# The norm and the transposes of the second block's first half of the tokens, with its first weights, between the steps of the last down product

## The chip, the cores and the metric

The kernel runs on one core of a Trainium2 chip. Its time is that of one execution on the device, in microseconds (us). Five engines work from queues of their own and wait for each other on semaphores: TensorE (PE, with its weight loads as PEld), VectorE (DVE), ScalarE (ACT), GpSimd (POOL) and SyncE (SP). DMA transfers are issued from the queues of SP, ACT and POOL.

## The reference

Two transformer blocks over 1024 tokens with 1024 channels, in float32. At the place of the change the first block ends and the second begins:

```python
def first_block(x, ...):
    ...
        u = rmsnorm(h, norm_mlp_g[l]) @ w_up[l]
        h = h + jnp.square(jax.nn.relu(u)) @ w_down[l]
    return rmsnorm(h, norm_final_g)

def second_block(x, ln1_g, w_in, b_in, ...):
        h = rms_norm(x, ln1_g[l])
        z = h @ w_in[l] + b_in[l]
        q, k, v, u, y_branch, g_att, g_rec = jnp.split(z, SPLITS, axis=-1)
        ...
        u = centred_depthwise_conv(u, conv_w[l], conv_b[l])
        ...
        y_rec = ((h_fwd + h_bwd) * jax.nn.gelu(y_branch)) @ w_rec_o[l]
        mixed = jax.nn.sigmoid(g_att) * y_att + jax.nn.sigmoid(g_rec) * y_rec
        x = x + mixed @ w_out[l]
        h2 = rms_norm(x, ln2_g[l])
        x = x + jnp.square(jax.nn.relu(h2 @ w_ff1[l])) @ w_ff2[l]
    return rms_norm(x, lnf_g)
```

So two norms meet: the first block's last one gives x1, the residual of the second block, and the second block's first one gives what is multiplied with w_in.

## The kernel before

A float32 product is made of three TensorE products: each operand is split into a high part, which ACT makes (`split`, L128, or L131 with a factor), and a low part, the rest, which DVE makes (L129, L132); the low part of some weights is made by POOL (`b.wlo`). High by high, high by low and low by high are added up in a PSUM bank.

The down product of the feed-forward (`ff_down`) is computed with 7 block products instead of 8 (in the manner of Strassen), each of 16 steps. A step multiplies a 128x512 left part with a 128x512 right part in four tiles q of 128 tokens: 12 matmuls. `divide(n)` splits the parts of a step, two steps ahead, into a ring of three buffers a side (tag `part`). The last three steps of the last product are done tile by tile, so that the tiles end one after the other; their parts have places of their own (`last_parts`). What a product gives is added to the eight token tiles `h` (128 tokens x 1024) by DVE between the steps of the next (L1066). The last product gives its four sums to the first half of the channels of tokens 4 to 7 only; these additions are kept in `b.late`, and `finish` calls them later. Tokens 0 to 3 are therefore complete some steps into the last product.

`block2` then makes the norms, four tokens at a time. Per token ACT squares and sums (L1350), DVE multiplies by norm_final_g (`gf`, L1335), ACT squares and sums again (L1353). Both root factors come from `rsqrt`, Newton steps on 128x4 tiles on DVE (L247 to L258). One factor (`rr`) scales h into `xn` (DVE, L1364), the other (`r1`) makes x1 in place (ACT, L1365), which goes to DRAM for later. `to_T` transposes `xn` on TensorE, two tokens at a time, by way of the banks `tp` and `sc`, and splits the transposed piece into `xT`, scaled by ln1_g. For tokens 4 to 7 this is put into the background list and drained between y and u of the first half.

The first projections are `y_chunk(0)` (the branch through GELU) and `u_chunk(0)` (which goes to the recurrence), each once for tokens 0 to 3 (js = 0) and once for 4 to 7 (js = 1); each makes two outputs of 24 matmuls. Later comes a list of other chunks, the attention, the recurrence, the merge of both branches, and a second feed-forward with the same `ff_down`.

The scheduler orders instructions by priority as they are written; `high_priority(offset)` lets some come earlier, `issue_after` holds some behind a given instruction.

## Time and profile before

| what | value |
|---|---|
| three runs | 3052.94, 3053.9, 3058.38 us |
| median | 3053.9 us |
| profiled execution | 3052.53 us, span 3050.8 us |
| TensorE busy | 2900.2 us, 95% of the span |
| DVE busy | 2162.9 us, 71% |
| ACT busy | 1231.9 us, 40% |
| mean granted TensorE clock | 0.977 of full speed |

The span goes from the first to the last instruction of the profiled execution. A busy TensorE is not TensorE at its peak, since its clock changes: 1.0 is 2.4 GHz, 0.5 is 1.2 GHz. In the span the last down product of the first block runs from about 1451.3 to 1494.9 us, and the first chunk of projections of the second block ends at about 1584 us.

### The profile page before, as it was taken

What the parts mean: (1) busy time and instruction counts of PE and PEld (TensorE: products, weight loads), DVE (VectorE), ACT (ScalarE), POOL (GpSimd) and SP (SyncE); (2) the same over time, 40 slices, a digit from 0 to 9 for tenths busy, and PEclk for the clock granted to TensorE, in tenths of its full rate; (3) what the DMA queues carried; (4) which work ended last, traced back from release to release, by engine and by line L of the source; (5) the groups of instructions that cost most, each with busy time, mean ns of one, the idle gap of its engine ahead of it and who ended that gap; (6) DMA issues with size and microseconds to landing.
All of it is one profiled execution on the core that took longest, in us unless ns stands there. A gap on an engine that the chain in (4) does not pass through costs nothing.

```text
span 3050.8 us, 40049 instructions
## 1 busy us (share of the span) xinstructions
PE 2900.2 (95%) x14596; PEld 2440.8 (80%) x14596; DVE 2162.9 (71%) x3903; ACT 1231.9 (40%) x2272; POOL 369.5 (12%) x402
## 2 busy tenths in 40 slices
PE   7898899999999999999699999999999999999997
PEld 5798788788877788888577789888788878888886
DVE  6997777565587776996558787643445777669976
ACT  4122566242253223444556664543311432224444
POOL 2240110000012431000111222200000011100000
PEclk9999899999999999999899999999999999999999
DMA  3225564211124768642211323477843233366522
GB/s 127 61 79 161 176 193 123 97 42 55 44 103 158 231 205 319 224 156 78 96 68 49 125 89 111 154 201 225 283 150 97 97 105 111 112 234 246 186 90 83
DMA packets 252501, 422.86 MB, mean 139 GB/s; under 512 B 27893, under 2 KB 130832, under 8 KB 252304
## 3 DMA queue, kind: packets, MB, share of 16 engines
q1 hardware_dynamic: 214240, 305.86, 31.2%
q0 software_dynamic: 28832, 95.57, 9.1%
q10 hardware_dynamic: 9232, 18.88, 1.6%
q8 instruction: 115, 1.88, 0.3%
q14 instruction: 82, 0.67, 0.1%
HBM read 310.75 MB, written 111.69 MB: 138 GB/s over the span
## 4 chain that ended last, share of the span: by engine, by line
PE 79%; DVE 10%; DMA 4%; ACT 3%; issue 2%; POOL 1%; SPq 0%; DVEq 0%; ACTq 0%; POOLq 0%
PE fd L1179 20%; PE mm L206 18%; PE ff L1007 15%; PE mm L177 5%; PE mm L179 5%; PE mm L178 5%; DVE acc L421 2%; PE ff L990 2%; PE pv L667 2%; PE tp L733 2%; PE pv L1641 1%; PE tp L240 1%; POOL w L129 1%; DMA bt<-rpb_d 1%; ACT w L128 1%
## 5 line engine op out<-in xcount | busy, mean ns | idle before, releaser
L1179 PE MATMUL fd<-part,part 128*128 128x512 f32 x2688 | 613.2, 390 | 1.0 <-DVE part L129 1.0
L1179 PEld LDWEIGHTS fd<-part,part 128*128 128x128 f32 x2688 | 503.5, 188 | 110.3 <-DVE part L129 5.9
L1007 PE MATMUL ff<-x,w 128*128 128x512 f32 x2352 | 541.6, 392 | 13.0 <-ACT w L128 7.3
L206 PE MATMUL mm<-xh,w 128*128 128x512 f32 x1792 | 532.2, 394 | 1.5 <-ACT lruC L1513 1.3
L1007 PEld LDWEIGHTS ff<-x,w 128*128 128x128 f32 x2352 | 443.7, 189 | 110.6 <-ACT w L128 9.0
L206 PEld LDWEIGHTS mm<-xh,w 128*128 128x128 f32 x1792 | 336.7, 189 | 70.1 <-ACT lruC L1513 2.4
L128 ACT ACTIVATE part<-keep 128x512 fp32r<-128x512 f32 x384 | 223.8, 623 | 252.0 <-PE fd L1179 247.4
L206 PE MATMUL mm<-xl,w 128*128 128x512 f32 x896 | 316.5, 393 | 0.0
L129 DVE TENSOR_TENSOR part<-keep,part 128x512 fp32r<-128x512 f32 x384 | 249.2, 683 | 47.2 <-ACT part L128 47.0
L128 ACT ACTIVATE w<-raw 128x1024 fp32r<-128x1024 f32 (+1 forms) x132 | 134.9, 1033 | 282.6 <-PE mm L178 111.5
L129 POOL TENSOR_TENSOR w<-raw,w 128x1024 fp32r<-128x1024 f32 x56 | 170.9, 3056 | 493.7 <-ACT w L128 491.2
L206 PEld LDWEIGHTS mm<-xl,w 128*128 128x128 f32 x896 | 168.9, 189 | 33.6
L232 DVE TENSOR_TENSOR h<-h,mm 128x512 f32<-128x512 f32 x176 | 119.7, 685 | 78.7 <-PE mm L179 77.9
L421 DVE SCALAR_TENSOR_TENSOR acc<-u,conv_wh,acc 128x1023 f32<-128x1023 f32 (+14 forms) x120 | 172.6, 1477 | 3.1 <-ACT acc L416 1.3
L177 PE MATMUL mm<-w,xh 128*128 128x256 f32 x512 | 147.9, 289 | 14.9 <-DVE u L447 11.5
L850 DVE TENSOR_TENSOR t2k<-ff,t2k 128x512 f32<-128x512 f32 x140 | 96.3, 688 | 82.1 <-PE ff L1007 80.8
L178 PE MATMUL mm<-w,xh 128*128 128x256 f32 x512 | 147.0, 287 | 0.0
L179 PE MATMUL mm<-w,xl 128*128 128x256 f32 x512 | 146.8, 287 | 0.0
L128 ACT ACTIVATE w<-wr 128x512 fp32r<-128x512 f32 x156 | 94.3, 630 | 119.6 <-PE ff L1007 55.8
L972 POOL DMA_DIRECT2D hid_d<-t2k x128 | 69.8, 545 | 488.9 <-DVE t2k L850 256.0
L129 DVE TENSOR_TENSOR w<-raw,w 128x1024 fp32r<-128x1024 f32 (+1 forms) x76 | 89.2, 1179 | 47.1 <-ACT w L128 47.0
L129 DVE TENSOR_TENSOR w<-wr,w 128x512 fp32r<-128x512 f32 x156 | 104.4, 686 | 15.8 <-ACT w L128 14.0
(355 smaller groups left out, 5167.5 us busy)
## 6 DMA issues: line engine op xcount, KB each, us to landing
hid_d<-t2k POOLq DMA_DIRECT2D x128, 256.0 KB, 3.0
x<-hid_d SPq DMA_DIRECT2D x128, 256.0 KB, 4.4
keep<-hid_d SPq DMA_DIRECT2D x96, 256.0 KB, 6.0
raw<-in_w_in_dram SPq DMA_DIRECT2D x40, 512.0 KB, 3.7
qk_d<-t2k SPq DMA_DIRECT2D x64, 256.0 KB, 2.6
wr<-in_w_up_dram SPq DMA_DIRECT2D x32, 512.0 KB, 3.8
keep<-in_w_down_dram SPq DMA_DIRECT2D x64, 256.0 KB, 5.2
wr<-in_w_ff_dram SPq DMA_DIRECT2D x32, 512.0 KB, 3.6
```

The costliest lines, as they stand in the source:

```text
L128: nc.scalar.activation(hi, src, AF.Copy)
L129: (eng or nc.vector).tensor_tensor(out=lo, in0=src, in1=fp(hi), op=ALU.subtract)
L177: nc.tensor.matmul(ps, sh, mh, start=(i == 0), stop=False)
L178: nc.tensor.matmul(ps, sh, ml, start=False, stop=False)
L179: self.last = nc.tensor.matmul(ps, sl, mh, start=False, stop=(i == n - 1))
L206: self.last = nc.tensor.matmul(pj[j], a, b, start=(k == 0 and q == 0), stop=(k == nk - 1 and q == 2))
L232: self.added[t] = self.nc.vector.tensor_tensor(out=hs, in0=hs, in1=ps, op=ALU.add)
L421: nc.vector.scalar_tensor_tensor(out=acc[m][:, lo:hi], in0=u[m][:, lo + d : hi + d], scalar=w(k), in1=acc[m][:, lo:hi], op0=ALU.mult, op1= ...
L850: tt = lambda o, x, y, op: nc.vector.tensor_tensor(out=o, in0=x, in1=y, op=op)
L972: stored.append(nc.gpsimd.dma_start(out=hid[2 * c + f, :, j * 512 : (j + 1) * 512], in_=o))
L1007: b.last = nc.tensor.matmul(ps, l[:, k, :], r, start=(opens and k == 0 and q == 0), stop=(k == 3 and q == 2), skip_group_check=True)
L1179: last = nc.tensor.matmul(ps[q], l[:, sl], r, start=(c == 0 and x == 0), stop=(c == C - 1 and x == 2))
```

## The change

The norm of `block2` becomes a class, `Front`, whose parts are called at given steps of the last product, by a table `work` that `ff_down` takes: the load of gf and of the first weights four steps ahead of the product; the squares of token q at step q + 1; the roots at step 5; the scaling of token q at step q + 6; the transposes of channel block k, two blocks a step at steps 10 to 12, and blocks 6 and 7 behind tiles 0 and 1 of the last three steps; the splits of the first weights of y at steps 11 and 12. A transposed piece now holds four tokens (128x512 instead of 128x256), so there are 8 rounds per half instead of 16. The scaling works in place on h; x1 goes into slots of its own and is stored from the GpSimd queue instead of ACT's. gf and the first weights are loaded from the GpSimd queue instead of SP's. The parts of the last three steps lie in `k2` to `k7`. For tokens 4 to 7, `rest` makes the norm behind the product, and the transposes (`turns`) are written behind y and u of js = 0, where before they stood between y and u.

```diff
@@ -237,7 +237,8 @@
     def transposes(self, dst, srcs):
         for i, s in enumerate(srcs):
-            self.nc.tensor.transpose(dst[:, i * P : (i + 1) * P], s, self.ident)
+            last = self.nc.tensor.transpose(dst[:, i * P : (i + 1) * P], s, self.ident)
+        return last
     def rsqrt(self, v, n=1):
...
@@ -1159,13 +1161,14 @@
             divide(n + PART)
         if len(steps) - LAST <= n + LAST < len(steps):
             if not last_parts:
-                last_parts += [b.slot(q, (P, 2, 512), F32R, "part") for q in (24, 25, 30)]
                 last_parts += [
-                    b.kpool.tile([P, 2, 512], F32R, tag=f"k{q}", name=b.nm("part")) for q in (0, 1, 8)
+                    b.kpool.tile([P, 2, 512], F32R, tag=f"k{q}", name=b.nm("part")) for q in range(2, 8)
                 ]
             divide(n + LAST)
         if n < 0:
             continue
+        for fn in work.get(n - len(steps) + C, ()):
+            fn(h)
         p, c = steps[n]
         if c == 0:
             ps = [
@@ -1191,6 +1194,8 @@
                     for m in range(n, len(steps)):
                         last = products(m, q, steps[m][1])
                 b.last = last
+                for fn in work.get(("tile", q), ()):
+                    fn(h)
         if c == C - 1:
             def evac(q, i, j, ps=ps):
...
-def block2(b, h):
-    nc, i = b.nc, b.i
-    tt = lambda o, a, q, op: nc.vector.tensor_tensor(out=o, in0=a, in1=q, op=op)
-    stt = lambda o, a, s, q, p0, p1: nc.vector.scalar_tensor_tensor(out=o, in0=a, scalar=s, in1=q, op0=p0, op1=p1)
-    b.x1_d = b.dram.tile([S, D], F32, name="x1_d")
-    gf = b.slot(11, name="gf")
-    nc.sync.dma_start(out=gf, in_=i["norm_final_g"].partition_broadcast(P))
-    xT = b.halves(range(0, 8))
-    last = None
-    for g0 in range(0, NT, 4):
-        ys = []
-        v, rr = (b.small(8, n) for n in ("bv", "br"))
-        for q in range(4):
-            t = g0 + q
-
-            finish(b, t, last)
-            junk = b.t2k((P, 1024), BF16)
-            nc.scalar.activation(junk, h[t], AF.Square, accum_out=v[:, q : q + 1])
-            last = tt(h[t], h[t], gf, ALU.mult)
-            junk = b.t2k((P, 1024), BF16)
-            nc.scalar.activation(junk, h[t], AF.Square, accum_out=v[:, 4 + q : 5 + q])
-        v0, v1, rr = v[:, 0:4], v[:, 4:8], rr[:, 0:4]
+class Front:
+    def __init__(self, b):
+        self.b, self.nc = b, b.nc
+        self.last = None
+        self.work = {}
+        for c, fn in (
+            [(-4, self.load)]
+            + [(q + 1, lambda h, q=q: self.squares(h, q)) for q in range(4)]
+            + [(5, lambda h: self.roots())]
+            + [(q + 6, lambda h, q=q: self.scaled(h, q, (25, 28, 29, 30)[q])) for q in range(4)]
+            + [(10 + k // 2, lambda h, k=k: self.turn(h, 0, k, (b.sc, b.pv))) for k in range(6)]
+            + [(11 + q, lambda h, q=q: self.weight(q)) for q in range(2)]
+            + [(("tile", k - 6), lambda h, k=k: self.turn(h, 0, k, (b.sc, b.pv))) for k in (6, 7)]
+        ):
+            self.work.setdefault(c, []).append(fn)
+    def load(self, h):
+        b, nc = self.b, self.nc
+        b.x1_d = b.dram.tile([S, D], F32, name="x1_d")
+        self.gf = b.slot(24, name="gf")
+        nc.gpsimd.dma_start(out=self.gf, in_=b.i["norm_final_g"].partition_broadcast(P))
+        self.xT = b.halves(range(8, 16))
+        self.w, self.raw = [], []
+        for q in range(2):
+            self.raw.append(b.kpool.tile([P, 4, 256], F32, tag=f"k{q}", name=b.nm("raw")))
+            nc.gpsimd.dma_start(
+                out=self.raw[q],
+                in_=b.i["w_in_2"][0, q * 512 : (q + 1) * 512, 2560:2816].rearrange("(k p) n -> p k n", p=P),
+            )
+    def weight(self, q):
+        b = self.b
+        hi, lo = (b.slot(26 + 2 * q + s, (P, 4, 256), F32R, "w") for s in range(2))
+        b.split(hi, lo, self.raw[q])
+        self.w.append((hi, lo))
+    def weights(self, k, c0, c1):
+        hi, lo = self.w[k // 4]
+        return hi[:, k % 4, c0:c1], lo[:, k % 4, c0:c1]
+    def squares(self, h, t):
+        b, nc, q = self.b, self.nc, t % 4
+        if q == 0:
+            self.v, self.rr = (b.small(8, n) for n in ("bv", "br"))
+        junk = lambda: b.slot(25 if t < 4 else 4 + q, (P, 1024), BF16, "junk")
+        nc.scalar.activation(junk(), h[t], AF.Square, accum_out=self.v[:, q : q + 1])
+        self.last = nc.vector.tensor_tensor(out=h[t], in0=h[t], in1=self.gf, op=ALU.mult)
+        nc.scalar.activation(junk(), h[t], AF.Square, accum_out=self.v[:, 4 + q : 5 + q])
+    def roots(self):
+        b, nc = self.b, self.nc
+        tt = lambda o, a, q, op: nc.vector.tensor_tensor(out=o, in0=a, in1=q, op=op)
+        v0, v1, rr = self.v[:, 0:4], self.v[:, 4:8], self.rr[:, 0:4]
         nc.vector.tensor_scalar(out=v0, in0=v0, scalar1=1.0 / D, scalar2=EPS, op0=ALU.mult, op1=ALU.add)
-        r1 = b.rsqrt(v0, 4)
+        r1 = self.r1 = b.rsqrt(v0, 4)
         tt(rr, r1, r1, ALU.mult)
         tt(rr, rr, v1, ALU.mult)
         nc.vector.tensor_scalar(out=v1, in0=rr, scalar1=1.0 / D, scalar2=EPS, op0=ALU.mult, op1=ALU.add)
         tt(rr, b.rsqrt(v1, 4), r1, ALU.mult)
-        for q in range(4):
-            t = g0 + q
-            y = b.slot(12 + t if t < 4 else 22 + t, name="xn")
-            last = nc.vector.tensor_scalar(out=y, in0=h[t], scalar1=rr[:, q : q + 1], scalar2=None, op0=ALU.mult)
-            nc.scalar.activation(h[t], h[t], AF.Copy, scale=r1[:, q : q + 1])
-            nc.scalar.dma_start(out=b.x1_d[t * P : (t + 1) * P, :], in_=h[t])
-            ys.append(y)
-        for g in (g0, g0 + 2):
-            if g < 4:
-                with b.tc.issue_after(b.last.ins):
-                    b.to_T(ys[g : g + 2], g, b.g_ln1, xT)
-            else:
-                b.bg.append((0, lambda ys=ys[g - 4 : g - 2], g=g: b.to_T(ys, g, b.g_ln1, xT, 100)))
-    xT += b.halves(range(8, 16))
+    def scaled(self, h, t, at):
+        b, nc, q = self.b, self.nc, t % 4
+        x1 = b.slot(at, name="x1")
+        nc.scalar.activation(x1, h[t], AF.Copy, scale=self.r1[:, q : q + 1])
+        nc.gpsimd.dma_start(out=b.x1_d[t * P : (t + 1) * P, :], in_=x1)
+        nc.vector.tensor_scalar(out=h[t], in0=h[t], scalar1=self.rr[:, q : q + 1], scalar2=None, op0=ALU.mult)
+    def turn(self, h, j, k, banks):
+        b = self.b
+        ps = banks[k % 2]()
+        with b.tc.issue_after(b.last.ins):
+            b.last = b.transposes(ps, [y[:, k * P : (k + 1) * P] for y in h[4 * j : 4 * j + 4]])
+        b.split(*self.xT[j][k], ps, scale=b.g_ln1[:, k : k + 1])
+    def rest(self, h):
+        b = self.b
+        for t in range(4, NT):
+            finish(b, t, self.last)
+            self.squares(h, t)
+        self.roots()
+        for t in range(4, NT):
+            self.scaled(h, t, t)
+        def turns():
+            self.xT += b.halves(range(0, 8))
+            with b.tc.high_priority(offset=100):
+                for k in range(KT):
+                    self.turn(h, 1, k, (b.sc, b.tp))
+        return turns
+def block2(b, h, front):
+    nc, i = b.nc, b.i
+    tt = lambda o, a, q, op: nc.vector.tensor_tensor(out=o, in0=a, in1=q, op=op)
+    stt = lambda o, a, s, q, p0, p1: nc.vector.scalar_tensor_tensor(out=o, in0=a, scalar=s, in1=q, op0=p0, op1=p1)
+    turns = front.rest(h)
+    xT = front.xT
     b.wlo = nc.gpsimd
     w_in = i["w_in_2"][0]
...
@@ -1432,10 +1499,10 @@
         while step not in done:
             b.bg.popleft()[1]()
-    ws = {}
+    ws = {("y", 0): front.weights}
     def y_chunk(q, js=(0, 1)):
-        if js[0] == 0:
+        if js[0] == 0 and q:
             ws["y", q] = b.w_s(w_in[:, 2560 + q * 256 : 2560 + q * 256 + 256])
         for mm in range(2):
             m = 2 * q + mm
@@ -1559,9 +1626,9 @@
     b.banks = 3
     for js in ((0,), (1,)):
         y_chunk(0, js)
+        u_chunk(0, js)
         if js == (0,):
-            b.drain()
-        u_chunk(0, js)
+            turns()
     seq = [0, y_chunk, u_chunk, 0, y_chunk, 0, u_chunk, 0, y_chunk, 0, u_chunk] + [0] * (1 + 4)
     others = [(qk_chunk, p) for p in range(4)] + [(v_chunk, n) for n in range(2)] + [(gate_chunk, q) for q in range(4)]
     nth = {y_chunk: 1, u_chunk: 1}
@@ -1756,10 +1823,11 @@
         if stop not in ("mix",):
             cross_part(b, h)
         if stop not in ("mix", "cross"):
-            h = ff_part(b, h, b.g_mlp, ins["w_up"][0], ins["w_down"][0], bias_tables(b))
+            front = Front(b)
+            h = ff_part(b, h, b.g_mlp, ins["w_up"][0], ins["w_down"][0], bias_tables(b), front.work)
             b.layout(None)
         if stop not in ("mix", "cross", "ff"):
-            block2(b, h)
+            block2(b, h, front)
             h = merge_part(b)
         if stop is None:
             h = ff_part(b, h, b.g_ln2, ins["w_ff1_2"][0], ins["w_ff2_2"][0])
```

The first place is the end of DVE's work for the last product (`part` are its splits, `h_11250` to `h_11253` tokens 0 to 3, `sm` the root factors). Before, with all splits of the product already ahead of these rows:

```order
L1335 TENSOR_TENSOR sm_13787<-sm_13827,sm_13809 128x4
L1364 TENSOR_SCALAR xn_13843<-h_11250,sm_13787 128x1024
L1364 TENSOR_SCALAR xn_13847<-h_11251,sm_13787 128x1024
L1364 TENSOR_SCALAR xn_13851<-h_11252,sm_13787 128x1024
L1364 TENSOR_SCALAR xn_13855<-h_11253,sm_13787 128x1024
L1066 TENSOR_TENSOR h_11254<-h_11254,fd_13458 128x512
L132 SCALAR_TENSOR_TENSOR xl_13782<-sc_13864,cols_412,xh_13778 128x256
```

After:

```order
L1393 TENSOR_TENSOR sm_13500<-sm_13626,sm_13608 128x4
L1408 TENSOR_SCALAR h_11250<-h_11250,sm_13500 128x1024
L1408 TENSOR_SCALAR h_11251<-h_11251,sm_13500 128x1024
L129 TENSOR_TENSOR part_13706<-x_13598,part_13706 128x512
L129 TENSOR_TENSOR part_13709<-keep_11232,part_13709 128x512
L1408 TENSOR_SCALAR h_11252<-h_11252,sm_13500 128x1024
L129 TENSOR_TENSOR part_13730<-x_13654,part_13730 128x512
L129 TENSOR_TENSOR part_13733<-keep_11232,part_13733 128x512
L1408 TENSOR_SCALAR h_11253<-h_11253,sm_13500 128x1024
L129 TENSOR_TENSOR part_13754<-x_13679,part_13754 128x512
L129 TENSOR_TENSOR part_13757<-keep_11233,part_13757 128x512
L129 TENSOR_TENSOR w_13849<-raw_13386,w_13848 128x1024
```

The four scalings now stand among the splits of steps 10 (`part_13706`, `part_13709`), 11 and 12, in front of the part of a weight split that DVE makes; the additions of tokens 4 to 7 have moved behind.

The second place is TensorE between the product and the transposes (`fd` are the product's four banks, `ident` marks a transpose). Before, the end of the product's last tile:

```order
L1179 MATMUL fd_13461<-part_13677,part_13676 128x512 x3
L1179 MATMUL fd_13461<-part_13675,part_13674 128x512 x3
L1179 MATMUL fd_13461<-part_13673,part_13672 128x512 x3
L240 MATMUL sc_13864<-ident,xn_13843 128x128
L240 MATMUL sc_13874<-ident,xn_13843 128x128
L240 MATMUL sc_13864<-ident,xn_13847 128x128
L240 MATMUL sc_13874<-ident,xn_13847 128x128
L240 MATMUL sc_13884<-ident,xn_13843 128x128
```

After, the end of step 9 and the start of step 10 of the same product:

```order
L1182 MATMUL fd_13475<-part_13685,part_13682 128x512 x3
L1182 MATMUL fd_13476<-part_13685,part_13682 128x512 x3
L240 MATMUL sc_13770<-ident,h_11250 128x128
L240 MATMUL sc_13770<-ident,h_11251 128x128
L240 MATMUL sc_13770<-ident,h_11252 128x128
L240 MATMUL sc_13770<-ident,h_11253 128x128
L240 MATMUL pv_13777<-ident,h_11250 128x128
L240 MATMUL pv_13777<-ident,h_11251 128x128
L240 MATMUL pv_13777<-ident,h_11252 128x128
L240 MATMUL pv_13777<-ident,h_11253 128x128
L1182 MATMUL fd_13473<-part_13709,part_13706 128x512 x3
L1182 MATMUL fd_13474<-part_13709,part_13706 128x512 x3
```

Blocks 0 and 1 of all four tokens stand between two steps; blocks 2 and 3, and 4 and 5, do the same a step later each.

The third place is ACT in the norm of tokens 4 to 7 (`sm` here are the sums of squares; `w_` with `raw_` is the high part of a weight). Before:

```order
L1353 ACTIVATE t2k_13945,sm_13939<-h_11254 128x1024
L1350 ACTIVATE t2k_13948,sm_13939<-h_11255 128x1024
L131 ACTIVATE xh_13778<-tp_13859,cols_412 128x256
L128 ACTIVATE w_14377<-raw_14374 128x1024
L1353 ACTIVATE t2k_13951,sm_13939<-h_11255 128x1024
L131 ACTIVATE xh_13779<-tp_13869,cols_412 128x256
L1350 ACTIVATE t2k_13954,sm_13939<-h_11256 128x1024
L131 ACTIVATE xh_13780<-tp_13879,cols_412 128x256
L128 ACTIVATE w_14384<-raw_14381 128x1024
L1353 ACTIVATE t2k_13957,sm_13939<-h_11256 128x1024
```

After:

```order
L1389 ACTIVATE junk_13939,sm_13928<-h_11255 128x1024
L1387 ACTIVATE junk_13942,sm_13928<-h_11256 128x1024
L128 ACTIVATE w_14080<-raw_14078 128x1024
L128 ACTIVATE w_14086<-raw_14084 128x1024
L1389 ACTIVATE junk_13945,sm_13928<-h_11256 128x1024
L1387 ACTIVATE junk_13948,sm_13928<-h_11257 128x1024
L1518 ACTIVATE t2k_14036<-mm_14011,cols_412 128x512
L1519 ACTIVATE t2k_14037<-mm_14011,cols_412 128x512
L128 ACTIVATE w_14329<-raw_14326 128x1024
L1389 ACTIVATE junk_13951,sm_13928<-h_11257 128x1024
L1522 ACTIVATE t2k_14037<-t2k_14037 128x512
L128 ACTIVATE w_14336<-raw_14333 128x1024
```

The splits of transposed pieces (L131) have left this stretch. The two passes over the first output of y (L1518, L1519) and a weight split (`w_14329`) stand now in front of the second square of the last token (`junk_13951`).

## Rows read from the trace of the kernel before

**Rows 1.** page part 1: engine, busy us (share of the span), instructions

```profile
PE 2900.2 (95%) x14596; PEld 2440.8 (80%) x14596; DVE 2162.9 (71%) x3903; ACT 1231.9 (40%) x2272; POOL 369.5 (12%) x402
```

**Rows 2.** windows: us, busy per engine (instructions), PEclk, DMA share, GB/s

```profile
1451.30:1494.90 43.60, 43.58 (x193) 35.75 (x191) 21.53 (x31) 20.56 (x36) 0.54 (x1) 1.00 0.22 70
1494.87:1533.81 38.94, 8.57 (x29) 4.11 (x28) 25.91 (x54) 25.73 (x44) 14.59 (x7) 0.56 0.33 111
1584.00:1960.00 376.00, 367.15 (x1777) 308.41 (x1776) 278.99 (x264) 226.59 (x279) 90.92 (x41) 0.99 0.31 99
```

**Rows 3.** windows of five us: same columns

```profile
1495.00:1500.00 5.00, 0.00 (x0) 0.00 (x0) 1.64 (x1) 3.33 (x6) 4.62 (x2) 0.96 0.23 57
1535.00:1540.00 5.00, 5.00 (x21) 4.11 (x20) 4.07 (x23) 1.78 (x4) 0.00 (x0) 0.79 0.26 90
```

**Rows 4.** chain that ended last, 1480 to 1565: start, us, what

```profile
1479.92 14.29 PE fd L1179 x63
...
1494.24 2.00 ACT w L128 x2
...
1498.36 2.76 DVE h L1335
...
1502.43 2.35 DVE sm L248
...
1510.78 2.74 DVE xn L1364 x4
```

**Rows 5.** timeline of ACT, 1472 to 1495: start, us, what [idle before]

```profile
1475.88 0.63 ACT L128 ACTIVATE part<-x 128x512 fp32r<-128x512 f32 x1 [1.57 <-PE fd L1179]
1476.42 0.62 ACT L128 ACTIVATE part<-keep 128x512 fp32r<-128x512 f32 x1
...
1479.66 1.04 ACT L1350 ACTIVATE t2k<-h 128x1024 bf16<-128x1024 f32 x1
1480.61 0.19 ACT L1350 ACTIVATION_READ_ACCUMULATOR t2k<-h 128x1 f32 x1
```

**Rows 6.** timeline of DVE, 1472 to 1528

```profile
1476.55 0.69 DVE L129 TENSOR_TENSOR part<-x,part 128x512 fp32r<-128x512 f32 x1 [1.43 <-ACT part L128]
1477.16 0.69 DVE L129 TENSOR_TENSOR part<-keep,part 128x512 fp32r<-128x512 f32 x1
...
1480.83 1.23 DVE L1335 TENSOR_TENSOR h<-h,gf 128x1024 f32<-128x1024 f32 x1 [0.27 <-ACT t2k L1350]
...
1510.58 0.16 DVE L1335 TENSOR_TENSOR sm<-sm,sm 128x4 f32<-128x4 f32 x1
...
1526.87 0.68 DVE L1066 TENSOR_TENSOR h<-h,fd 128x512 f32<-128x512 f32 x1
```

**Rows 7.** timeline of POOL, 1494 to 1540

```profile
1495.38 4.65 POOL L129 TENSOR_TENSOR w<-raw,w 128x1024 fp32r<-128x1024 f32 x2 [7.82 <-ACT w L128]
1502.39 4.70 POOL L129 TENSOR_TENSOR w<-raw,w 128x1024 fp32r<-128x1024 f32 x2 [2.36 <-ACT w L128]
1526.69 2.36 POOL L129 TENSOR_TENSOR w<-raw,w 128x1024 fp32r<-128x1024 f32 x1 [19.60 <-ACT w L128]
```

**Rows 8.** timeline of ACT, 1494 to 1592

```profile
1511.56 1.15 ACT L1365 ACTIVATE h<-h,sm 128x1024 f32<-128x1024 f32 x1 [6.89 <-DVE xn L1364]
...
1583.95 0.69 ACT L1471 ACTIVATE u<-mm,cols 128x512 f32<-128x512 f32 x1 [3.47 <-PE mm L206]
```

**Rows 9.** chain, 1541 to 1556: a transpose pair at full clock

```profile
1546.45 0.22 PE tp L240 x2
```

**Rows 10.** DMA view: issues, KB each, median us to landing

```profile
h_d<-h POOLq DMA_DIRECT2D x16, 512.0 KB, 3.0
...
x_d<-h ACTq DMA_DIRECT2D x8, 512.0 KB, 2.6
...
raw<-in_w_in_dram POOLq DMA_DIRECT2D x8, 512.0 KB, 4.2
```

**Rows 11.** PE's waits, 1960 to 2240: us, times, longest

```profile
PE mm L206 <- DVE ev L1699: 4.9, 1, 4.9
```

6 lines of the change are left out of this document (3 added, 3 removed).

## The prediction

> **What bounds the kernel now.** I read the page's first part first: TensorE is busy 95% of the span [rows 1], so the kernel is a queue of matmuls and only places where TensorE stands still, or runs slowly, can give much. The windows show where. In the last down product TensorE is busy 43.58 of 43.60 us at full clock [rows 2]: 16 steps of 2.725 us, 192 matmuls of 0.227 us. Then comes the hole: from 1494.87 to 1533.81 it is busy 8.57 of 38.94 us at a mean clock of 0.56 [rows 2]. Behind it the projections of the second block run dense, 367 of 376 us [rows 2].
>
> The chain of waits says what fills the hole [rows 4]. The last product ends; a weight split that has waited for it holds ACT for 2.0 us; the rest of the norm of tokens 0 to 3 follows (the gain product, the roots, four scalings of 0.69 us); then transposes and splits take turns, then all that again for tokens 4 to 7. The first chunk's four outputs per half (y 0, y 1, u 0, u 1) are done when ACT takes the last of them at 1583.95 [rows 8]. So from the end of the product to there it is 1583.95 - 1494.87 = 89.1 us. The work in it that only TensorE can do is 192 matmuls x 0.227 = 43.6 us and 64 transposes x 0.11 [rows 9] = 7.0 us. What is left, 38.5 us, is the most that this place can return.
>
> **The change, part by part.** *First half of the norm.* ACT and DVE are busy 20.6 and 21.5 of the last product's 43.6 us [rows 2], so there is room. ACT gets 8 square passes of 1.14 [rows 5] and 4 copies of 1.15 [rows 8], 13.7 us; DVE gets 4 gain products of 1.23, 29 small operations that start 0.20 apart, and 4 scalings of 0.69 [rows 4, 6], 13.5 us; the first weights add two splits (ACT 1.0 each [rows 4], DVE about 1.2). That fits in sum, but the order of the rows decides. A step's split can start when the step three before it has ended (three buffers), and costs a pair on ACT of 1.16 and on DVE of 1.30 [rows 5, 6], together 2.0 us; it is needed 5.45 us after its start is allowed. Laying out the new rows of both engines with these durations, the splits of steps 2 to 9 are ready 0.7 to 1.9 us before TensorE wants them. So I charge nothing there; the cover is thin, and each us by which ACT runs later beyond it is a us of TensorE.
>
> *The first stall.* Eight transposes now stand between step 9 and step 10, and they need all four scaled tokens. Step 9 ends at 1451.3 + 10 x 2.725 = 1478.55. In my layout DVE has done step 9's split at 1475.2; then come 19 small operations x 0.20 = 3.8, two scalings 1.4, the split pair of step 10, 1.3, a scaling 0.7, the pair of step 11, 1.3, a scaling 0.7: 1484.4. The stall is then 5.8 us. If DVE were not behind at step 9 (ready 2.0 us after its buffers come free at 1470.4), all of it would be 2.8 us earlier: 3.0 us. I take 5.0, nearer the late end, since the order puts squares and three early splits of the last steps ahead of step 9's. Step 10's split is done before that, so it adds nothing.
>
> *The clock.* The mean granted clock was 0.96 in 1495 to 1500, with TensorE idle from 1494.87: at half speed for 0.4 us of the five, so it fell some 4.7 us after the last matmul. In 1535 to 1540 it was 0.79, so it was back after 2.1 us there, 3.3 us after dense work began at 1533.81 [rows 3]. A fall thus costs 3.3 / 2 = 1.7 us. A stall of 5.0 is on the edge; I charge 1.0, with 0 and 1.7 as bounds.
>
> *Transposes in the product.* 32 x 0.11 = 3.5 us, wholly added to the product, since TensorE was full there. Their splits (ACT and DVE 0.7 each) have one step or one tile of cover; k 4 waits for a bank that k 0's split frees, which waits on ACT for a weight split, and this for stores of the x1 copies into whose slots it writes. Stores take 3.0 us from the GpSimd queue where the ACT queue takes 2.6 [rows 10]. They go out by 1480 and land by 1483, and k 4 is due at about 1491: covered.
>
> *First chunk, first half.* 96 matmuls x 0.227 = 21.8 us can follow the product at once, since weights and transposed tokens are there.
>
> *The second stall.* Tokens 4 to 7 get their last addition only when the product's tiles end, and their norm must fit into these 21.8 us. Count from the product's end. ACT reaches the first square of token 7 at about 5.2 (two weight splits stand before it), then the two passes over the first output, which TensorE has ready at 5.4, then a split of u's zero-padded weights whose load can only start when POOL has finished another weight (5.5) and takes 3 to 4 us: so token 7's second square ends at 11.4. Of the 29 small operations 15 to all wait for it, 3.0 to 5.8 us; I take 4.2. But POOL now runs its two subtractions of 2.36 us beside them. Before, a gain product that started during POOL's pair took 2.76 instead of 1.23 us, and a pair of tiny operations 2.35 [rows 4, 6, 7]; an addition that reads the product's bank kept its 0.68 us while POOL worked [rows 6, 7]. So operations on SBUF alone wait for POOL's end, up to 5 us in all, and 4.5 with the part that lies before 11.4; three GELU operations (2 us) and four scalings (2.8) end at 24.9. The stall is 24.9 - 21.8 = 3.1 us. Without the meeting with POOL it is 0; with later loads, up to 8 and a fall of the clock. I take 3.0.
>
> *The rest.* 32 transposes 3.5, 96 matmuls 21.8. Moving gf and the first weights to the GpSimd queue takes loads off SP that nothing waited for; the x1 stores leave ACT's queue. The order of SP changes much later too, in the merge, where TensorE has a wait of 4.9 us for a late load's product [rows 11]: loads for it now stand earlier. Bounds 0 and 4.9, or 2 lost if it only moves; I take 2.
>
> **Sum.** 5.0 + 1.0 + 3.5 + 21.8 + 3.0 + 3.5 + 21.8 = 59.6 us against 89.1: 29.5 us less, and 2 more in the merge. The profiled execution took 3052.5 us, 1.4 under the median of 3053.9: 3052.5 - 31.5 + 1.4 = 3022.4, say **3022 us**.
>
> **Rivals.** (A) Neither stall: DVE is not late, POOL's work passes between. 38.5 us go: 3015. For it: in sum the engines have room; against it: all four scaled tokens are needed at once. (B) Both stalls are wide and each lets the clock fall: 5.8 + 1.7 + 8 + 1.7 = 17.2 us where I have 9.0: 3030, up to 3034 if the merge loses. For it: thin cover, and the chain of loads and POOL. (C) The gain is given back: what follows is 98% TensorE [rows 2], which speaks against it, but the merge waits for memory; if half is lost there, 3037, and if all, no change.
>
> (D) DVE also makes POOL wait. By the rows, POOL's operations kept 2.33 and 2.36 us [rows 7] while DVE's stretched, so I had POOL unhindered. If the one that comes first holds the other off, two gain products of 1.23 would delay POOL's subtractions, and the load behind them, by 2.5 us: the second stall is 5.5, 3024.5. The Trainium skill, "SBUF — State Buffer", section "Who interferes with whom", says this: the engine that issues first has the shared port pair for its whole instruction, and the other is fully blocked. The rows agree for DVE; none shows POOL waiting.
>
> (E) Slower. ACT's second square of token 0 stands ahead of step 3's split and waits for gf, whose slot comes free after the additions for step 1, eight steps ahead: about 1432. A load from this queue lands in 4.2 us [rows 10], 17 us before its use at 1453. Each us beyond 17 stops ACT, then TensorE; it decides when gf lands 50 us after its issue.
>
> **Chances.** Forecast (3017 to 3027) 0.54, A 0.14, B 0.14, C 0.07, D 0.07, E 0.04. The range reaches from A's time with the merge's gain, 3012, to B's, 3033; C's and E's tail and the rest of A and B stay outside. A measurement of this kernel tells about 0.2%, 6 us, from no change. Faster by more: all but E and half of C, 0.93; within: 0.03; slower 0.04.
>
> **What would show it.** A product of about 53 us with an idle stretch of 3 to 6 us after its step 9, ended by a scaling on DVE; no idle before the first chunk; small DVE operations of 2 us beside POOL some 13 to 18 us after the product; a stall of 0 to 8 us before the second half's transposes. Waits for splits in steps 2 to 9 would mean that my layout is too kind, and a gap over 8 us in either place, or new waits behind 1584, that the forecast is wrong.

## The result, and the profile after

The changed kernel took 3017.14 us (median of four runs, 3006.57 to 3019.88), the kernel before 3053.82 us (median of four). The ratio is 0.9862, 95% interval 0.9848 to 0.9875. The medians differ by 36.7 us; 0.9862 of 3053.8 would be 3011.7, 42 us less (38 to 46). The forecast was 3022 us, 31.5 less, with a range from 3012 to 3033. The profiled execution took 3015.72 us (span 3013.9), 36.8 less than that of before.

One execution differs from the next by several us wherever the program waits for memory, so what the change does is read from a stretch of the profile: from the first matmul of the first block's down projection to the first matmul of the q and k chunk, which follows the first chunk of y and u. Its ends, in the trace of before (the first line: duration, count, first and last start of the product's matmuls; the second: the timeline, where the pattern of three high parts in a row begins):

```profile
L1179 PE MATMUL fd<-part,part x2688: 387/389/504, 1187.8 to 3033.5; 128*128 128x512 f32 x192
```

```profile
1583.52 0.84 PE L206 MATMUL mm<-xh,w 128*128 128x512 f32 x3
```

and in that of after:

```profile
L1182 PE MATMUL fd<-part,part x2688: 387/389/775, 1185.6 to 2996.5; 128*128 128x512 f32 x192
```

```profile
1549.58 0.84 PE L206 MATMUL mm<-xh,w 128*128 128x512 f32 x3
```

That is 1583.52 - 1187.8 = 395.7 us before and 1549.58 - 1185.6 = 364.0 us after: 31.7 less. Each was profiled a second time, and the stretch came out at 395.5 and 363.8 us, while its start moved from 1187.8 to 1182.4 us and from 1185.6 to 1192.7 us: the transition repeats to 0.2 us, while the first block, which the change does not touch, shifts by 5 to 7 us from one execution to the next.

The windows of after, from the start of the last product to its end and on to the end of the first chunk, answer to [rows 2]:

```profile
1449.10:1500.76 51.66, 49.09 (x225) 40.44 (x224) 38.77 (x78) 35.80 (x60) 2.71 (x5) 0.97 0.29 99
1500.76:1549.58 48.82, 47.54 (x225) 39.14 (x224) 31.77 (x61) 28.69 (x42) 13.19 (x9) 1.00 0.23 79
```

The hole of 38.9 us with TensorE busy for 8.6 at a clock of 0.56 is gone: 51.7 us for the product with the first half's transposes, 48.8 us for the first chunk with the second half's.

The first wait, on TensorE's timeline (start, us, what, and the idle time before it with what ended it):

```profile
1476.16 0.38 PE L240 MATMUL sc<-ident,h 128*128 128x128 f32 x2
1477.57 0.33 PE L240 MATMUL sc<-ident,h 128*128 128x128 f32 x1 [1.03 <-DVE h L1408]
1479.43 0.33 PE L240 MATMUL sc<-ident,h 128*128 128x128 f32 x1 [1.54 <-DVE h L1408]
...
1480.16 4.40 PE L1182 MATMUL fd<-part,part 128*128 128x512 f32 x12
...
1485.19 3.00 PE L1182 MATMUL fd<-part,part 128*128 128x512 f32 x12
```

and the scalings on VectorE that it waits for:

```profile
1469.99 0.69 DVE L129 TENSOR_TENSOR part<-keep,part 128x512 fp32r<-128x512 f32 x1
...
1474.22 1.42 DVE L1408 TENSOR_SCALAR h<-h,sm 128x1024 f32<-128x1024 f32 x2
...
1476.76 0.75 DVE L1408 TENSOR_SCALAR h<-h,sm 128x1024 f32<-128x1024 f32 x1
...
1478.63 0.75 DVE L1408 TENSOR_SCALAR h<-h,sm 128x1024 f32<-128x1024 f32 x1
```

TensorE comes to the transposes at 1476.2, finds two of the four tokens scaled, and waits 1.03 and 1.54 us for the other two, which stand behind the splits of steps 10 and 11. The step behind it then takes 4.40 us where the next takes 3.00. The granted clock says why (windows, same columns as above):

```profile
1480.00:1482.50 2.50, 2.50 (x9) 2.02 (x8) 2.50 (x4) 1.18 (x2) 0.00 (x0) 0.50 0.57 185
1482.50:1485.00 2.50, 2.50 (x14) 2.10 (x13) 0.54 (x1) 0.00 (x0) 0.00 (x0) 0.87 0.79 275
```

Half clock for 2.5 us, and in the next 2.5 us for a quarter of them: with the end of the window before, some 3.4 us, 1.7 lost.

The second half's norm, on VectorE, GpSimd and ScalarE:

```profile
1507.10 2.98 DVE L1388 TENSOR_TENSOR h<-h,gf 128x1024 f32<-128x1024 f32 x1 [2.15 <-ACT junk L1387]
...
1511.93 2.56 DVE L249 TENSOR_TENSOR sm<-sm,sm 128x4 f32<-128x4 f32 x2
...
1514.72 2.51 DVE L249 TENSOR_TENSOR sm<-sm,sm 128x4 f32<-128x4 f32 x2
...
1523.27 1.40 DVE L1408 TENSOR_SCALAR h<-h,sm 128x1024 f32<-128x1024 f32 x2
```

```profile
1504.13 4.87 POOL L129 TENSOR_TENSOR w<-raw,w 128x1024 fp32r<-128x1024 f32 x2 [11.48 <-ACT w L128]
1511.86 2.41 POOL L129 TENSOR_TENSOR w<-raw,w 128x1024 fp32r<-128x1024 f32 x1 [2.87 <-DMA raw<-in_w_in_dram]
...
1514.81 2.40 POOL L129 TENSOR_TENSOR w<-raw,w 128x1024 fp32r<-128x1024 f32 x1
```

```profile
1510.73 1.06 ACT L128 ACTIVATE w<-raw 128x1024 fp32r<-128x1024 f32 x1 [2.51 <-DMA raw<-in_w_in_dram]
1511.69 1.04 ACT L1389 ACTIVATE junk<-h 128x1024 bf16<-128x1024 f32 x1
```

A gain product that began beside GpSimd's pair took 2.98 us, two pairs of 128x4 operations 2.56 and 2.51 us where a pair alone takes 0.36 (at 1511.34), ending 0.22 and 0.02 us behind a GpSimd operation; GpSimd's own kept 2.41 and 2.40. ScalarE stood still for 2.51 us for a weight's load, in front of the last token's second square (whose input, that gain product, was ready only at 1510.08). TensorE waits little for all that:

```profile
1524.07 0.33 PE L240 MATMUL sc<-ident,h 128*128 128x128 f32 x1 [0.94 <-DVE h L1408]
1524.73 0.33 PE L240 MATMUL sc<-ident,h 128*128 128x128 f32 x1 [0.33 <-DVE h L1408]
```

0.94 and 0.33 us, and the clock stays at full speed.

Later, in the merge, the stretch from the last pv matmul of the neighbourhood attention to the first matmul of the output product; before:

```profile
L1641 PE MATMUL pv<-nV,pt x384: 243/275/330, 1998.2 to 2150.7; 128*128 128x96 f32 x192
```

```profile
L177 PE MATMUL mm<-w,mix x128: 388/389/497, 2258.8 to 2402.2; 128*128 128x512 f32 x128
```

after:

```profile
L1708 PE MATMUL pv<-nV,pt x384: 243/275/330, 1964.9 to 2117.3; 128*128 128x96 f32 x192
```

```profile
L177 PE MATMUL mm<-w,mix x128: 388/389/497, 2221.7 to 2365.1; 128*128 128x512 f32 x128
```

2258.8 - 2150.7 = 108.1 us before and 2221.7 - 2117.3 = 104.4 after. TensorE's waits there (sum, times, longest) were, beside the 4.9 us of [rows 11]:

```profile
PE mm L206 <- ACT ev L1423: 1.5, 1, 1.5
PE mm L206 <- DVE t2k L1699: 1.0, 1, 1.0
```

and are in the trace of after:

```profile
PE mm L206 <- DVE ev L1766: 3.3, 4, 1.2
PE mm L206 <- DVE t2k L1766: 1.6, 2, 1.0
```

So the waits went from 7.4 to 4.9 us, 2.5 less. The other 1.2 us are busy time of TensorE (100.75 us before, 99.55 after): the mean granted clock of the stretch was 0.97 before and 1.00 after.

### The profile page after: what moved, and what is told of

Read it like the earlier page. It is cut to its first block, busy times and chain, and to the rows that moved or that the text cites. A ratio compares the mean times of both kernels' runs of the same rounds, so it can differ in the third digit from the quotient of the medians.

```text
span 3013.9 us, 40030 instructions
## 1 busy us (share of the span) xinstructions
PE 2895.5 (96%) x14596; PEld 2438.7 (81%) x14596; DVE 2162.4 (72%) x3889; ACT 1227.5 (41%) x2256; POOL 379.2 (13%) x411
## 3 DMA queue, kind: packets, MB, share of 16 engines
q1 hardware_dynamic: 213040, 304.29, 31.5%
## 4 chain that ended last, share of the span: by engine, by line
PE 78%; DVE 9%; DMA 5%; ACT 3%; issue 2%; POOL 2%; SPq 1%; DVEq 0%; ACTq 0%; POOLq 0%
PE fd L1182 19%; PE mm L206 18%; PE ff L1009 15%; PE mm L177 5%; PE mm L179 5%; PE mm L178 5%; PE ff L992 2%; PE pv L668 2%; PE tp L734 2%; POOL w L129 1%; PE pv L1708 1%; PE tp L240 1%; DMA bt<-rpb_d 1%; ACT w L128 1%; DVE w L129 1%
## 5 line engine op out<-in xcount | busy, mean ns | idle before, releaser
L177 PE MATMUL mm<-w,xh 128*128 128x256 f32 x512 | 147.9, 289 | 13.5 <-ACT t2k L470 10.3
```

The costliest lines, as they stand in the source:

```text
L177: nc.tensor.matmul(ps, sh, mh, start=(i == 0), stop=False)
```

## The experiments

All with the stretch of above, the merge (from the last pv matmul to the first output product) and the median of the timed runs. They were run in four sets, in which the kernel before had medians of 3053.8, 3055.9, 3055.7 and 3057.8 us:

| kernel | first fd | first q, k | stretch us | merge us | median us |
|---|---|---|---|---|---|
| before | 1187.8 | 1583.52 | 395.7 | 108.1 | 3053.8 |
| before, again | 1182.4 | 1577.90 | 395.5 | 108.2 | 3049.7 (one run) |
| after | 1185.6 | 1549.58 | 364.0 | 104.4 | 3017.1 |
| after, again | 1192.7 | 1556.53 | 363.8 | 104.3 | 3017.5 |
| turns one step later | 1188.9 | 1548.69 | 359.8 | 103.8 | 3017.9 |
| q, k weights late | 1185.1 | 1547.21 | 362.1 | 103.5 | 3013.9 |
| both late | 1186.4 | 1544.73 | 358.3 | 104.0 | 3014.4 |
| norm written behind | 1189.2 | 1548.64 | 359.4 | 104.6 | 3015.6 |
| first weights behind | 1191.3 | 1561.69 | 370.4 | 103.7 | 3025.6 |
| turns between y and u | 1190.3 | 1560.45 | 370.2 | 104.0 | 3027.2 |
| before, scratch in a slot | 1187.1 | 1560.82 | 373.7 | 109.3 | 3034.3 |
| norm behind, scratch in the pool | 1186.1 | 1555.54 | 369.4 | 104.3 | 3022.8 |
| stores of x1 from ScalarE | 1184.0 | not readable | see below | 103.8 | 3024.1 |
| norm behind, q, k weights late | 1193.1 | 1550.58 | 357.5 | 104.4 | 3011.8 |

The medians differ by some us where the stretches say nothing of it (3017.9 for 359.8 us, 3017.1 for 364.0), so the stretch decides between variants of the changed kernel.

**The same kernels again.** No edit.

> The changed kernel once more, to see how much of its time differs from one execution to the next and where. In its first profile the stretch from the start of the last product to the end of the first chunk took 100.4 us against 132.6 before, 32.2 less; 2.2 us were gained before that stretch, in code that the change does not touch, and 2.5 behind it. Theory: the transition repeats to within 0.5 us, and what differs between executions (3006.6 to 3019.9 us) lies before 1200 us of the span, in the first block. Rival: the executions differ in the transition itself, by the meeting of VectorE with GpSimd or by the stores; then the 100.4 us move by several us.

> The kernel before once more, with a profile. Theory: the transition takes 132.6 us again to within 0.5, and the first product of the down projection starts at another time than 1187.8 us, by up to some us, as between the two profiles so far (1187.8 and 1185.6). Rival: it starts at 1187.8 to within 0.3 us again; then the 2.2 us that the changed kernel gains ahead of the transition belong to the change.

The theory held: the transition repeats, and the first fd matmul starts anywhere from 1182.4 to 1193.1 us over these profiles, in either kernel. What the changed kernel gained ahead of the transition in its first profile, 2.2 us, is chance.

**Transposes one step later.**

```diff
-            + [(10 + k // 2, lambda h, k=k: self.turn(h, 0, k, (b.sc, b.pv))) for k in range(6)]
+            + [(11 + k // 2, lambda h, k=k: self.turn(h, 0, k, (b.sc, b.pv))) for k in range(4)]
-            + [(("tile", k - 6), lambda h, k=k: self.turn(h, 0, k, (b.sc, b.pv))) for k in (6, 7)]
+            + [(("tile", k - 4), lambda h, k=k: self.turn(h, 0, k, (b.sc, b.pv))) for k in (4, 5, 6, 7)]
```

> The transposes of the first half stand one step later: two channel blocks each ahead of steps 11 and 12, and one behind each of the four last tiles. In the changed kernel TensorE waited 2.6 us for the scalings between step 9 and step 10, and ran at half clock for 3.4 us after it (1.7 us lost). Theory: the scalings are done 2.7 us earlier relative to the transposes, so the wait and the fall of the clock both vanish: 4.3 us less than the changed kernel, and the product takes 47.1 us. Rival 1: the wait only moves to the start of the first chunk, since the last block's split comes behind the last tile: 0 to 2 us less. Rival 2: the clock falls because of the transposes themselves, wait or no wait: 2.6 us less, with a granted clock of 0.5 behind the first transposes.

4.2 us less against 4.3 expected. Both rivals fell: the transposes follow without a wait, the step behind them takes 2.99 us, and only step 10's own split is a little late:

```profile
1480.33 2.83 PE L1182 MATMUL fd<-part,part 128*128 128x512 f32 x11 [0.44 <-DVE part L129]
...
1483.79 2.99 PE L1182 MATMUL fd<-part,part 128*128 128x512 f32 x12
```

**The q and k weights behind the second half's transposes.** Their splits are issued behind the last split of a transposed piece on ScalarE.

```diff
     def qk_chunk(p):
-        w = b.w_s(w_in[:, p * P : p * P + P], w_in[:, 512 + p * P : 512 + p * P + P])
+        with ExitStack() if p else b.tc.issue_after(front.turned.ins):
+            w = b.w_s(w_in[:, p * P : p * P + P], w_in[:, 512 + p * P : 512 + p * P + P])
...
                 for k in range(KT):
                     self.turn(h, 1, k, (b.sc, b.tp))
+            self.turned = b.last_scaled
```

> The weight splits of the first q and k chunk, which stood on ScalarE in front of the second square of the last token and gave GpSimd its two subtractions of 2.4 us beside the roots, are held behind the splits of the second half's transposed pieces. Theory (the second wait is made by these: a load that ScalarE waits for, 2.5 us, and two GpSimd operations that hold the small operations of VectorE, 2.2 us each): the scalings are done 4 to 6 us earlier and the wait of about 2.0 us ahead of the second half's transposes is gone; 2.0 us less than the changed kernel, and the operations L249 take 0.36 us for two throughout. Rival: ScalarE's copies or the GELU operations take the place, and the wait stays at 1 us or more.

1.9 us less, and TensorE goes into the transposes without a wait:

```profile
1521.96 0.60 PE L240 MATMUL sc<-ident,h 128*128 128x128 f32 x4
```

Both edits together:

> Both edits at once: the first half's transposes one step later and the splits of the first q and k weights behind the second half's transposes. From the start of the last product to the first matmul of the q and k chunk the changed kernel took 100.4 us; the two edits alone took about 4.0 and 1.9 us off. Theory: they act at different places and add: 94.5 us. Rival: with the first wait gone, ScalarE reaches the second half's squares at the same time relative to the product's end, so nothing is shared and they add as well, but the clock or a weight split fills one of them again: 96 us or more. The whole time is blurred by about 5 us from execution to execution.

They add, 5.7 us of 6.1; the stretch ends at 94.8 us against 94.5.

**The same work, written behind the product.** The table's calls are made in `block2`, in the same order; the load of gf and the first weights stays ahead.

```diff
-        for fn in work.get(n - len(steps) + C, ()):
+        for fn in (work.get(n - len(steps) + C, ()) if n - len(steps) + C == -4 else ()):
             fn(h)
...
                 b.last = last
-                for fn in work.get(("tile", q), ()):
-                    fn(h)
...
+    for c in list(range(16)) + [("tile", q) for q in range(4)]:
+        for fn in front.work.get(c, ()):
+            fn(h)
     turns = front.rest(h)
```

> Everything of the change except its place in the program: gf and the first weights are loaded as in the change, but squares, roots, scalings, transposes and weight splits of the first half are written behind the product. The scheduler moves the norm's ScalarE and VectorE work up between the splits by itself, and leaves the transposes behind the last tile. Theory A (the gain comes from the early loads and from places of their own for junk, parts and x1, which let the norm run ahead; where the transposes stand matters little): the product takes 43.6 us, the transposes of the first half follow at once and are half hidden, and the whole stretch takes 98 to 102 us, as in the changed kernel. Theory B (it comes from the explicit places between the steps): the norm runs late, a hole of 10 us or more opens behind the product, the clock falls, and the stretch takes over 108 us.

Theory A, and more: 359.4 us, 4.6 less than with the transposes between the steps. They start when the last tile ends, at 1496.11, with nothing to wait for, since the norm is done by then; the second half waits 1.2 us in sum:

```profile
1496.11 0.60 PE L240 MATMUL sc<-ident,h 128*128 128x128 f32 x4
...
1521.89 0.30 PE L240 MATMUL sc<-ident,h 128*128 128x128 f32 x1 [0.28 <-DVE h L1406]
```

So it is not the place of the transposes between the steps that pays. Two experiments ask what does.

**The squares' scratch tiles.** The sum of squares is all that is wanted of a square pass; its elements go to a scratch tile. The kernel before takes it from the pool of small tiles (`t2k`), and the change from a slot. First the kernel before with a slot for it:

```diff
-            junk = b.t2k((P, 1024), BF16)
+            junk = b.slot(26, (P, 1024), BF16, "junk")
             nc.scalar.activation(junk, h[t], AF.Square, accum_out=v[:, q : q + 1])
...
-            junk = b.t2k((P, 1024), BF16)
+            junk = b.slot(26, (P, 1024), BF16, "junk")
             nc.scalar.activation(junk, h[t], AF.Square, accum_out=v[:, 4 + q : 5 + q])
```

> The kernel before with one thing altered: the squares' scratch tiles lie in a slot that the last product no longer uses, and not in the pool of small tiles, which takes the place of the product's ring of parts once this is done. The scheduler then puts the norm of tokens 0 to 3 between the splits of the last product by itself. The stretch from the first matmul of the down projection to the first of the q and k chunk took 395.7 and 395.5 us in the kernel before and 364.0 and 363.8 in the changed one. Theory (the late start of the squares was the main thing that held the transition up): the norm is done at the product's end, and the stretch takes 370 to 378 us, with what is left being the weights (6.5 us in the experiment with them behind) and the transposes between y and u (6.2 us). Rival: the weights, split behind the product, hold it up anyway: over 385 us. The order of SyncE's loads in the merge is that of the kernel before here: if that order is what gains 4 us there, the time from the last pv matmul of the neighbourhood attention to the first output product stays at 108 us.

373.7 us: 22.0 of the 31.7 us come with this alone, and nothing else of the change. Of what TensorE still waits for (sum, times, longest; 8.0 us in all) nothing is a weight, against the theory, and the longest wait stands ahead of the second half's transposes between y and u:

```profile
PE tp L240 <- DVE xn L1364: 4.4, 1, 4.4
...
PE mm L206 <- ACT xh L131: 0.6, 1, 0.6
```

Then the norm written behind the product, with its scratch back in the pool:

```diff
-        junk = lambda: b.slot(25 if t < 4 else 4 + q, (P, 1024), BF16, "junk")
+        junk = lambda: b.t2k((P, 1024), BF16)
```

> The kernel with the first half's work written behind the product, whose stretch took 359.4 us, with the squares' scratch tiles back in the pool of small tiles. Its order puts all squares behind the last split again. Theory: the squares begin 28 us into the last product and end 42 us into it, the scalings come 5 us after its end, TensorE waits for them and the clock falls (1.7 us): 366 to 370 us. Rival: the stretch stays within 2 us of 359.4, since roots and scalings run in the shadow of the product's last tiles.

369.4 us, 10.0 more. The first square runs at 1477.98, when the product's last split is done, 28 us after the product's start, and TensorE waits 5.98 us behind the product for the first scaled token:

```profile
1477.98 1.04 ACT L1385 ACTIVATE t2k<-h 128x1024 bf16<-128x1024 f32 x1
```

```profile
1499.17 0.47 PE L240 MATMUL sc<-ident,h 128*128 128x128 f32 x1 [5.98 <-DVE h L1406]
```

The order shows the same in the kernel before: its squares stand behind all splits [rows 5]. The pool of small tiles is opened when the pools of the down projection are closed, and gets its room from them; a tile of it must wait for the tiles whose room it takes. That the room is shared is read from the program; the two runs show what it costs. Which tile the scratch waits for is not shown. It is not the ring of parts, as the expectation has it: at 1477.98 the ring's three buffers a side still held steps 10 to 12 (the product began at 1449.6, so step 10 ran from 1476.9 to 1479.6).

The last kernel also shows what the scratch does not explain: with it back in the pool, 395.7 - 369.4 = 26.3 us of the gain are still there. The two ways overlap: the slot alone gives 22.0, the rest of the change without it 26.3, both 36.3 (the kernel with the norm written behind). In the kernel before, the squares do not only begin late; behind the third token's first square ScalarE then stops for the first weight split, which waits for the end of the product and stands in front of the three squares that are left:

```profile
1494.24 2.00 ACT L128 ACTIVATE w<-raw 128x1024 fp32r<-128x1024 f32 x2 [6.48 <-PE fd L1179]
```

Behind it VectorE's gain product and small operations run beside GpSimd's parts of these weights [rows 4, 7], and the scalings begin at 1510.78, 15.9 us behind the product's end. With the weights split early and the scratch in the pool ScalarE does not wait for the product's matmuls there, and the scalings begin at 1498.37, 5.2 us behind it. So the trace names the first weights as the second cause; the kernel before with early weights alone was not run.

**The two other parts.** The first weights loaded and split as before (in `y_chunk`, from SyncE's queue, into the common ring), the rest of the change kept:

```diff
-            + [(11 + q, lambda h, q=q: self.weight(q)) for q in range(2)]
...
-    ws = {("y", 0): front.weights}
+    ws = {}
...
-        if js[0] == 0 and q:
+        if js[0] == 0:
             ws["y", q] = b.w_s(w_in[:, 2560 + q * 256 : 2560 + q * 256 + 256])
```

> The first weights of y are loaded and split as in the kernel before (from SyncE's queue, into the common ring), the rest of the change stays. Theory: ScalarE splits them only behind the product, so the first chunk waits for split and subtraction, 5 to 8 us behind the product's end, with a fall of the clock of 1.7 us; the second half's norm then has more time, so its wait of 2.0 us is gone: 3 to 7 us more than the changed kernel's 100.4 us. Rival: the ring has a free place by then and the splits run inside the product: 100.4 us to within 1.

6.4 us more. TensorE waits behind the product for ScalarE's split and for GpSimd's part, its clock is at 0.50 from 1510 to 1515, and the second half's wait is gone, as the theory has it:

```profile
1509.64 0.52 PE L206 MATMUL mm<-xh,w 128*128 128x512 f32 x1 [3.16 <-ACT w L128]
...
1512.19 1.22 PE L206 MATMUL mm<-xh,w 128*128 128x512 f32 x2 [0.76 <-POOL w L129]
```

And the second half's transposes between y and u:

```diff
         y_chunk(0, js)
-        u_chunk(0, js)
         if js == (0,):
             turns()
+        u_chunk(0, js)
```

> The second half's transposes stand between y and u of the first half of the tokens again, as in the kernel before; the rest of the change stays. The scaled tokens 4 to 7 were ready 20.2 to 23.9 us behind the product's end in the changed kernel. In this kernel's order TensorE meets the first of these transposes some 14 us behind the product's end. Theory: it waits there about 6 us instead of 2.0 at the end, and the clock falls: 4 to 7 us more than the changed kernel's 100.4 us. Rival: the work that is left over (u of the first half) fills the later waits, so that the sum of the waits stays within 2 us of the changed kernel's.

6.2 us more, with the wait expected and the clock at 0.50 from 1525 to 1530:

```profile
1524.52 0.48 PE L240 MATMUL sc<-ident,h 128*128 128x128 f32 x1 [6.64 <-DVE h L1408]
```

**The stores of x1 from ScalarE's queue.**

```diff
-        nc.gpsimd.dma_start(out=b.x1_d[t * P : (t + 1) * P, :], in_=x1)
+        nc.scalar.dma_start(out=b.x1_d[t * P : (t + 1) * P, :], in_=x1)
```

> The changed kernel with the x1 copies stored from ScalarE's queue as in the kernel before. Theory: the queue matters only where somebody waits for the stores, the second weight split, which had 2 to 3 us to spare: the stretch stays at 364 us to within 0.5. Rival: issuing holds ScalarE 0.3 us for each of the four stores among the splits of steps 10 to 12, or GpSimd's descriptors had waited for VectorE's scalings: 1 us more or 1 to 2 us less.

Neither. The first wait is the same, 1.08 and 1.54 us, and the step behind it ran at full clock this time; the second wait grew: TensorE's waits for scalings sum to 6.2 us in place of 3.8, and the clock fell there.

```profile
1478.49 2.98 PE L1182 MATMUL fd<-part,part 128*128 128x512 f32 x12
...
1522.85 0.33 PE L240 MATMUL sc<-ident,h 128*128 128x128 f32 x1 [2.07 <-DVE h L1408]
```

```profile
1478.00:1480.00 2.00, 2.00 (x12) 1.75 (x13) 2.00 (x4) 1.67 (x3) 0.00 (x0) 1.00 0.51 189
1520.00:1525.00 5.00, 1.77 (x9) 1.39 (x10) 2.62 (x5) 4.37 (x7) 0.00 (x0) 0.93 0.68 280
1525.00:1530.00 5.00, 5.00 (x28) 4.40 (x27) 3.62 (x6) 3.37 (x6) 0.00 (x0) 0.72 0.09 34
```

In this trace the pattern by which the first q and k matmul is found does not show, so the stretch is read to the next mark behind it, the first matmul of the recurrence's gates (L177). From the first fd matmul to that one it took 1572.3 - 1184.0 = 388.3 us, in the two profiles of the changed kernel 386.0 and 385.8: 2.4 more. A scaling in place must wait for its token's copy (0.92 and 0.29 us here), and ScalarE's order is another one: the last two copies, at 1520.87, stand behind a GELU pass for which ScalarE waited 2.03 us for VectorE, and behind an output of u. That the stores' issue itself, 0.33 us each, delays them is not shown. This kernel's median was 3024.1 us.

**The best version.** The norm written behind the product and the q and k weights late.

> The first half's work written behind the product (the stretch took 359.4 us) with the splits of the first q and k weights behind the second half's transposes (1.8 us less in the changed kernel). Theory: TensorE's waits ahead of the second half's transposes, 1.2 us in the first of these kernels, go: 357.5 to 358.5 us, some 6 us less than the changed kernel. Rival: ScalarE is held by the splits of the transposed pieces behind the product, the second half's norm comes as late as before, and it stays at 359.4.

357.5 us, 6.5 less than the changed kernel and 38.2 less than before. In the transition TensorE does not wait, and its clock does not fall (windows around the second half's transposes):

```profile
1520.00:1525.00 5.00, 5.00 (x24) 4.14 (x23) 3.23 (x6) 1.58 (x2) 1.29 (x2) 1.00 0.80 322
1525.00:1530.00 5.00, 5.00 (x39) 4.31 (x38) 3.19 (x5) 4.49 (x8) 0.00 (x0) 1.00 0.00 0
```

Its median, 3011.8 us, is the lowest of all (ratio to before 0.9852, 0.9834 to 0.9871); the changed kernel's in another set of runs was 3017.5 (0.9867, 0.9851 to 0.9884), so on whole times the two cannot be told apart.

## Why the prediction was right or wrong

**What bounds.** Right. The 38.5 us that only waits and transposes in turns cost were there to be had: the best version takes 38.2 of them.

**The sum.** From the start of the last product to the end of the first chunk it gave 43.6 + 59.6 = 103.2 us; measured 100.5 (364.0 less the six products and the start ahead of it, 263.5), before 132.2. By its terms: first wait 5.0, measured 2.57; clock 1.0, measured 1.7; second wait 3.0, measured 1.27; transposes and matmuls 50.6, measured 0.7 more. The step that failed, in the term of the first wait, is the layout of ScalarE's and VectorE's rows in the last product. It had VectorE done with step 9's split 23.9 us into the product; it was at 21.6 us (the subtraction at 1469.99, product start 1449.1). From there to the last scaling it took 8.7 us where the layout has 9.2, and three transposes ran between the waits. So what came is close to the forecast's other branch, VectorE not late at step 9, for which it had 3.0 us but which it did not take. The rows of the layout are not in the forecast, so where it loses the 2.3 us stays open; in the trace the additions of tokens 0 to 3 began 0.8 us before the product (1448.30).

**The late splits.** Right that steps 2 to 9 are covered: no wait for a part of these steps.

**The clock.** The bound of 1.7 was right, the edge was not: a wait of 5 us was thought to be near the limit, and the clock fell after two waits that sum to 2.6 us, with four transposes among them, in two of the three profiles with these waits. That 1.0 and 1.7 lie near each other is in part luck: the 1.0 was charged for a wait twice as long.

**The second half.** Place and mechanism were right: token 7's second square ended 12.1 us behind the product's end (forecast 11.4) and the last scaling 23.9 (24.9), with GpSimd's operations holding VectorE's small ones at 11 and 14 us behind the product's end. The weight whose load ScalarE waits for was named wrongly: it is the q and k chunk's, not u's, and it need not stand there at all.

**The merge.** 2 us were charged, between 0 and 4.9; it gave 3.7 and 3.9 in the two pairs of profiles. That the wait named would be what goes is only partly so: the waits gave 2.5 and the clock 1.2. The kernel before with a slot for the scratch keeps the old order of SyncE's loads and took 109.3 us there; all kernels with the new order took 103.5 to 104.6. At the point where they part, four loads of the recurrence's result stand ahead of the next two gate loads in the old order, and two in the new. So the order goes with the time in all these kernels, but it was never changed alone, and why the scheduler chose another was not tried.

**The whole time.** By stages the change gives 31.7 + 3.8 = 35.5 us, 4 more than forecast; the medians say 36.7, the ratio of the runs 42 (38 to 46), and a second set 0.9867 (0.9851 to 0.9884), 41 us (35 to 46). The terms that were mis-sized are the two waits with the clock (9.0 us, measured 5.5), the merge (2, measured 3.8) and none for the blur between executions, in which the down projection begins anywhere in 11 us; the range's lower end left no room for it. Where 1 to 6 us more than the stages' sum would come from in the timed runs, which have no profile, stays open.

**Rivals.** (A) was the side on which it came out wrong, in part. (B), (C) and (E) did not come: gf was issued at 1405.4 us, not at about 1432 as (E) has it, and landed 5.9 us later, 39 us before its first use. (D): with one of GpSimd's operations beside VectorE at a time they kept 2.4 us; the first pair, 4.87 us where 4.65 and 4.70 stood before [rows 7], may have waited 0.2 us for a gain product that ended at 1504.35. The Trainium skill, "SBUF — State Buffer", section "Who interferes with whom", is borne out for VectorE (2.98 us for a gain product of 1.23), and no run here shows GpSimd blocked for a whole instruction.

**What the forecast missed** is the cause. It read the change as its words have it, work moved between the steps, and did not ask why the norm began so late before. The runs show two causes that overlap: where a scratch tile's room comes from (22.0 us alone, 10.0 when taken back last) and the other parts of the change (26.3 us without it), of which the trace points to the first weights, split ahead of the norm's chain. The scheduler places the norm between the steps by itself once nothing forbids it. The table's own places gave nothing more: its transposes cost 4.6 us against the same work written behind, and 0.4 when they stand one step later.

## What to carry to other kernels

Where an engine's work starts later than its inputs are there, look for what it writes to, before moving it by hand: a scratch tile from a pool that takes over the room of the stage before holds back everything behind it. Look also at what stands in front of it in its own queue: a weight split that waits for the end of the stage holds back what is ready. Work placed by hand between the steps of a full engine costs a wait and perhaps a fall of the clock when one input is late; behind the last step, or one step later, the same work found its inputs ready. Weights that nobody needs yet should not stand in front of a chain that somebody waits for, above all when their second half runs on GpSimd beside small VectorE operations.

## What the runs showed of the hardware

The same 2.6 us of waits between step 9 and step 10 brought TensorE's clock down to half in both profiles of the changed kernel, for about 3.4 us each, and not at all in the kernel with the stores on ScalarE's queue, whose waits there were 1.08 and 1.54 us. So such a wait costs 2.6 us, or 4.3 with the fall of the clock; what decides is not shown. Operations of 128x4 elements, 0.16 us each, were held for nearly the whole of GpSimd operations of 2.4 us: two pairs took 2.56 and 2.51 us in place of 0.36.
